# Whole normalized input and side-by-side in-projections in all later sub-layers of a two-layer decoder trunk

## The chip, the core and the metric

The kernel runs on one core of a Trainium2 chip. The metric is the device time of one execution in microseconds (us). The engines are named PE (TensorE, matmul; PEld is its weight load), DVE (VectorE), ACT (ScalarE), POOL (GpSimd) and SP (SyncE, which issues the loads).

## The reference

`x` is one sequence of 256 tokens with 1024 features, in float32. Two layers of three sub-layers each are applied, and a final RMSNorm. The sub-layers are numbered 0 to 5 in what follows.

```python
cond = silu(c)
for l in range(2):
    mod = cond @ ada_w[l] + ada_b[l]            # shift, scale, gate for each of 3 sub-layers
    h = rmsnorm(x, g) * (1 + scale) + shift     # modulate
    x = x + 0.5 * gate * swiglu(h)              # sub-layers 0 and 3: FFN, D_FF = 2816
    h = modulate(x)
    x = x + gate * (retention(h) if l == 0 else short_conv(h))   # sub-layers 1 and 4
    h = modulate(x)
    x = x + 0.5 * gate * swiglu(h)              # sub-layers 2 and 5: FFN
return rmsnorm(x, final_g)
```

`swiglu(h)` is `(silu(h @ w_gate) * (h @ w_up)) @ w_out`. `retention` projects to q, k, v and a gate, takes decayed scores of 4 heads against v, normalizes each head and multiplies by silu of the gate. `short_conv` multiplies two projections, filters the product with a causal 3-tap filter per feature, multiplies by a third projection and projects out.

## The kernel before

Features lie on the partitions: `x` is 8 blocks of 128 features x 256 tokens. Every float32 product is made exact enough by halves: `split_high` and `split_low` turn each load of weights (128 x 2048) into a high half (`hi`, an ACT cast, line 245) and a low half (`lo`, a subtraction on DVE or POOL, line 250), and the moving operand is split the same way. `product` then issues three half-products for each 128x128 weight block: hi x high, hi x low, lo x high. If the output is twice as wide as the operand (line 284), the first two are one matmul of 512 columns, whose two output halves are added later ("side by side", lines 285 and 289); otherwise they are two matmuls onto the same 256 columns (lines 287 to 289).

Every weight is used once, so the kernel is one stream of loads (SP queue), splits and matmuls. `weights()` keeps `AHEAD` = 4 loads in preparation; there are six `hi` and six `lo` tiles, two of each for a load. In between, 64 loads of `ada_w` are reduced on DVE (line 120) for the modulation of later sub-layers, paced so that they end in sub-layer 4. From the eleventh block of the first FFN on, the conditioning vector for these reductions lies in one of the four PSUM pairs (`kept`), which leaves three.

A later sub-layer does not wait for its own rms. `scaled` makes `h` = x * scale as soon as a residual is done, with the shift as two extra columns (so 258 columns, S1), and the first projection starts on `h`. `modulated` issues this first projection, then sums the squares over partitions with matmuls against ones (line 358), std on ACT (line 370) and r = 1/std on DVE (line 376). In the FFN and the short convolution all projections use `h`; `normalized` multiplies PSUM by r (line 325), and the shift enters behind it as a bias per feature. Only the retention makes the whole normalized input as well (`whole`: lines 437, 438, 331 and 332, x * r, scale and shift, split), into 8 tiles of the pool `slot`. Its first three projections (`BIASED`) use `h`, and all behind them use `whole`; its gates go side by side through `projected` (one half is copied by ACT, line 312, the other added by DVE, line 313).

The retention's `values` forms a head's four 128-feature blocks in two PSUM pairs, two blocks in each; `normalize` forms the rms of a head of one step earlier, and stands before `values` in the loop. For the first sub-layer `first_modulated` squares x in four pairs of blocks (line 476, three on DVE, one on POOL) and sums all eight blocks on PE. There the order on ACT, DVE and POOL is that of the program; elsewhere a scheduler orders each engine's instructions by program order and by the times at which it estimates that operands and buffers are ready.

## Time and profile before

| | us |
|---|---|
| median of 3 runs (lowest, highest) | 1095.13 (1094.88, 1095.41) |
| the profiled execution, its own time | 1094.71 |
| its span, first to last instruction | 1092.9 |
| PE busy in the span | 1067.8 |
| DVE busy | 830.8 |
| ACT busy | 578.0 |
| POOL busy | 391.0 |

The span is what the trace covers; the execution's own time has 1.8 us more around it. A PE that counts as busy may still be slower than it could be, since matmuls are pipelined and their bars overlap: its rate is read from the start times of matmuls that stand far apart.

### The profile page before, as it was taken

The page shows a single profiled execution, that of the slowest core. Times are in us where ns is not written, and L with a number is a line of the kernel's source. Part 1 is how long each engine was busy: PE and PEld are TensorE (multiplying, and loading weights), DVE is VectorE, ACT ScalarE, POOL GpSimd, SP SyncE. Part 2 cuts the span into 40 slices and gives each one's busy share as a digit, 9 for nine tenths or more (in the row PEclk, how much of TensorE's full clock was granted, in tenths as well). Part 3 has the DMA queues.
Part 4 walks back from the last instruction along what each step waited for, and adds up shares of the span by engine and source line. Part 5 has one row for each costly group of instructions (what it writes and reads, how often), then busy time and mean ns, then how long its engine had stood idle before and what let it go on. Part 6 is the DMA issues. An engine that isn't in the chain of part 4 may idle for free.

```text
span 1092.9 us, 19439 instructions
## 1 busy us (share of the span) xinstructions
PE 1067.8 (98%) x7706; PEld 1008.9 (92%) x7706; DVE 830.8 (76%) x1089; ACT 578.0 (53%) x923; POOL 391.0 (36%) x339
## 2 busy tenths in 40 slices
PE   8999999999998999999999999999999989999996
PEld 7999988999887889999988999998899989999985
DVE  6999776998558898887678878767798686666454
ACT  4364444663367655545555644545564484454442
POOL 0034355345354432332445133344411442323352
PEclk9999999999999999999999999999999999999998
DMA  9977779867555687777679767767885545553441
GB/s 344 364 275 275 295 280 314 314 239 296 208 221 198 227 308 274 268 277 261 219 267 324 300 249 297 266 223 264 305 317 210 190 156 191 173 188 123 156 133 39
DMA packets 44573, 268.51 MB, mean 246 GB/s; under 512 B 4801, under 2 KB 6977, under 8 KB 19906
## 3 DMA queue, kind: packets, MB, share of 16 engines
q1 hardware_dynamic: 43138, 266.56, 67.1%
q8 instruction: 60, 0.98, 0.4%
q10 hardware_dynamic: 1344, 0.71, 0.2%
q14 instruction: 31, 0.25, 0.1%
HBM read 266.20 MB, written 1.05 MB: 245 GB/s over the span
## 4 chain that ended last, share of the span: by engine, by line
PE 59%; DVE 2%; issue 0%; ACT 0%; DVEq 0%; ACTq 0%
PE ps L289 20%; PE ps L288 14%; PE ps L287 14%; PE ps L285 11%; DVE lo L250 1%; PE ps L358 0%; DVE rsum L511 0%; DVE h L412 0%; DVE raw L804 0%; DVE r L800 0%; DVE x L514 0%; ACT hi L245 0%; DVEq L877 0%; DVE x L516 0%; ACT std L370 0%
## 5 line engine op out<-in xcount | busy, mean ns | idle before, releaser
L250 DVE TENSOR_TENSOR lo<-raw,hi 128x1024 fp32r<-128x1024 f32 (+1 forms) x300 | 366.6, 1230 | 176.6 <-ACT hi L245 161.1
L245 ACT CAST hi<-raw 128x1024 fp32r<-128x1024 f32 (+2 forms) x408 | 377.7, 937 | 221.2 <-PE ps L288 123.3
L288 PE MATMUL ps<-h,hi 128*128 128x258 f32 (+1 forms) x1520 | 430.4, 283 | 1.7 <-DVE h L412 1.5
L287 PE MATMUL ps<-h,hi 128*128 128x258 f32 (+1 forms) x1520 | 430.5, 283 | 1.1 <-DVE sum L325 1.1
L289 PE MATMUL ps<-h,lo 128*128 128x258 f32 (+1 forms) x1520 | 430.5, 283 | 0.0
L250 POOL TENSOR_TENSOR lo<-raw,hi 128x384 fp32r<-128x384 f32 (+1 forms) x108 | 201.5, 1867 | 290.4 <-ACT hi L245 290.0
L288 PEld LDWEIGHTS ps<-h,hi 128*128 128x128 f32 x1520 | 288.7, 190 | 2.6 <-DVE h L412 1.3
L287 PEld LDWEIGHTS ps<-h,hi 128*128 128x128 f32 x1520 | 289.0, 190 | 1.8 <-ACT sg L586 0.7
L289 PEld LDWEIGHTS ps<-h,lo 128*128 128x128 f32 x1520 | 288.7, 190 | 0.0
L285 PE MATMUL ps<-act,hi 128*128 128x512 f32 x616 | 217.5, 398 | 0.6 <-DVE rsum L511 0.6
L289 PE MATMUL ps<-act,lo 128*128 128x256 f32 x704 | 197.8, 281 | 0.0
L332 POOL TENSOR_TENSOR act<-av,act 128x256 fp32r<-128x256 f32 x88 | 84.0, 957 | 251.2 <-ACT act L331 242.8
L120 DVE CUSTOM_DVE_ANT_0 raw<-raw,ps,misc 128x1024 f32<-128x1024 f32 x124 | 154.5, 1274 | 0.0
L285 PEld LDWEIGHTS ps<-act,hi 128*128 128x128 f32 x616 | 115.6, 188 | 29.4 <-DVE rsum L511 1.7
L289 PEld LDWEIGHTS ps<-act,lo 128*128 128x128 f32 x704 | 133.1, 189 | 0.3 <-DVE lo L250 0.3
L331 ACT CAST act<-av 128x256 fp32r<-128x256 f32 x88 | 35.5, 405 | 100.4 <-DVE av L590 78.3
L325 DVE TENSOR_TENSOR sum<-ps,r 128x516 f32<-128x516 f32 (+1 forms) x103 | 70.7, 690 | 16.1 <-PE ps L289 15.8
L590 DVE SCALAR_TENSOR_TENSOR av<-sum,sg 128x256 f32<-128x256 f32 x66 | 51.9, 786 | 17.8 <-ACT sg L589 17.8
L289 PE MATMUL ps<-whole,lo 128*128 128x256 f32 x208 | 58.5, 281 | 0.0
L589 ACT ACTIVATE sg<-sum 128x256 f32<-128x256 f32 x66 | 33.6, 509 | 26.3 <-DVE sum L325 25.9
L341 ACT ACTIVATE sq<-x 128x256 f32<-128x256 f32 x48 | 19.7, 416 | 51.6 <-DVE x L514 44.3
L348 POOL TENSOR_TENSOR acc<-acc,sq 128x256 f32<-128x256 f32 x32 | 28.0, 875 | 38.8 <-ACT sq L341 33.7
(132 smaller groups left out, 1296.2 us busy)
## 6 DMA issues: line engine op xcount, KB each, us to landing
raw<-in_ffn_in SPq DMA_DIRECT2D x80, 1024.0 KB, 4.9
raw<-in_ada_w SPq DMA_DIRECT2D x64, 1024.0 KB, 5.5
raw<-in_ffn_out SPq DMA_DIRECT2D x64, 704.0 KB, 4.2
raw<-in_ada_w SPq DMA_DIRECT2D x16, 512.0 KB, 6.8
raw<-in_ffn_in SPq DMA_DIRECT2D x16, 512.0 KB, 7.6
raw<-in_ret_g SPq DMA_DIRECT2D x8, 1024.0 KB, 5.1
raw<-in_ret_qk SPq DMA_DIRECT2D x8, 1024.0 KB, 5.1
raw<-in_ret_v SPq DMA_DIRECT2D x8, 1024.0 KB, 4.8
```

Source lines behind the costliest of these rows:

```text
L120: ins = nc.vector.tensor_tensor_reduce(out=w, in0=w, in1=state["cond"], scale=1.0, scalar=misc[:, C_ADAB + 72 * l + col:C_ADAB + 72 * l + ...
L245: nc.scalar.copy(out=hi, in_=raw[:, c:c + m])
L250: eng.tensor_tensor(out=lo, in0=raw, in1=hi, op=ALU.subtract)
L285: nc.tensor.matmul(out=ps, lhsT=hi, rhs=m.rearrange("p n s -> p (n s)"), start=start, stop=False)
L287: nc.tensor.matmul(out=ps, lhsT=hi, rhs=m[:, 0], start=start, stop=False)
L288: nc.tensor.matmul(out=ps, lhsT=hi, rhs=m[:, 1], start=False, stop=False)
L289: nc.tensor.matmul(out=ps[:, :n], lhsT=lo, rhs=m[:, 0], start=False, stop=stop)
L325: nc.vector.tensor_tensor(out=y[:, :, :n], in0=ps[:, :, :n], in1=r[:, :n].unsqueeze(1).to_broadcast([P, 2, n]), op=ALU.mult)
L331: hi = nc.scalar.copy(out=dst[:, 0], in_=src)
L332: lo = eng.tensor_tensor(out=dst[:, 1], in0=src, in1=dst[:, 0].bitcast(F32), op=ALU.subtract)
L589: nc.scalar.activation(out=sg, in_=y[:, 0, :S], func=AF.Silu, bias=y[:, 0, S:S + 1])
L590: nc.vector.scalar_tensor_tensor(out=av, in0=y[:, 1, :S], scalar=y[:, 1, S:S + 1], in1=sg, op0=ALU.add, op1=ALU.mult)
```

## The change

In all later sub-layers the whole normalized input is made, and every projection behind the third uses it side by side, without a bias. `ffn` and `short_conv` take the record `src` that the retention had, and go through `projected`. The pool `slot` grows from 22 to 30 tiles of 128 x 512; for that the scaled blocks of the first sub-layer (`xs`) come from it, and `cond` takes a tile of the pool of high halves. `values` puts a head's four blocks into one PSUM pair and is issued before the `normalize` of the head before. In the first sub-layer DVE and POOL each square two pairs, and pairs are added before PE sums them.

```diff
@@ -72,7 +72,7 @@
     wraw_p = ctx.enter_context(tc.tile_pool(name="wraw", bufs=5))
     whi_p = ctx.enter_context(tc.tile_pool(name="whi", bufs=6))
     wlo_p = ctx.enter_context(tc.tile_pool(name="wlo", bufs=6))
-    slot_p = ctx.enter_context(tc.tile_pool(name="slot", bufs=22))
+    slot_p = ctx.enter_context(tc.tile_pool(name="slot", bufs=30))
     xhl_p = ctx.enter_context(tc.tile_pool(name="xhl", bufs=1))
     tmp = ctx.enter_context(tc.tile_pool(name="tmp", bufs=2))
     psum = ctx.enter_context(tc.tile_pool(name="psum", bufs=4, space=bass.MemoryType.PSUM))
@@ -85,7 +85,7 @@
 
 
     misc = const.tile([P, C_END], F32, name="misc")
-    cond = const.tile([P, D], F32, name="cond")
+    cond = whi_p.tile([P, D], F32, name="cond", tag="hi")
     table = const.tile([P, T_END], F32, name="table")
     ones = const.tile([P, P], F32, name="ones")
     eps = const.tile([P, 1], F32, name="eps")
@@ -239,7 +239,7 @@
         c = w["done"]
         m = min(step, width - c)
         if c % SPLIT == 0:
-            hi, lo = whi_p.tile([P, SPLIT], F32R, name="hi"), wlo_p.tile([P, SPLIT], F32R, name="lo")
+            hi, lo = whi_p.tile([P, SPLIT], F32R, name="hi", tag="hi"), wlo_p.tile([P, SPLIT], F32R, name="lo")
             w["parts"].append((hi, lo))
         hi, lo = (part[:, c % SPLIT:c % SPLIT + m] for part in w["parts"][-1])
         nc.scalar.copy(out=hi, in_=raw[:, c:c + m])
@@ -471,17 +471,21 @@
             with tc.issue_after(conditioned.ins):
                 load_table(AF.Sqrt, ones)
             ps = banks()[:, 0, :S]
-            for i, pair in enumerate(x_pairs):
-                sq = tmp.tile([P, 2, S], F32, name="sq2", tag="rot" if i % 2 else "sum")
-                (nc.gpsimd if i == 1 else nc.vector).tensor_tensor(out=sq, in0=pair, in1=pair, op=ALU.mult)
-                total([sq[:, 0, :], sq[:, 1, :]], ps, i == 0, i == KB // 2 - 1)
+            for i in range(2):
+                sqs = []
+                for j, eng in ((2 * i, nc.vector), (2 * i + 1, nc.gpsimd)):
+                    sq = tmp.tile([P, 2, S], F32, name=f"sq{j}", tag="rot" if i else "sum")
+                    eng.tensor_tensor(out=sq, in0=x_pairs[j], in1=x_pairs[j], op=ALU.mult)
+                    sqs.append(sq)
+                (nc.gpsimd if i else nc.vector).tensor_tensor(out=sqs[0], in0=sqs[0], in1=sqs[1], op=ALU.add)
+                total([sqs[0][:, 0, :], sqs[0][:, 1, :]], ps, i == 0, i == 1)
             std = tmp.tile([P, S], F32, name="std")
             nc.scalar.activation(out=std, in_=ps, func=AF.Sqrt, bias=eps, scale=1.0 / D)
             fill(FILL)
             for k in range(KB):
                 ada_reduce(l, s, k, ada.pop(), True)
                 if k % 2 == 0:
-                    pair = tmp.tile([P, 2, S], F32, name=f"xs{k}", bufs=1)
+                    pair = in_halves(slot(F32, "xs"))
                 xs = pair[:, k % 2, :]
                 nc.scalar.activation(out=xs, in_=x[k], func=AF.Copy, scale=scale_t[l][s][:, k:k + 1])
                 raw, width, w = load(2)
@@ -574,30 +578,33 @@
                     nc.tensor.matmul(out=out, lhsT=lo, rhs=h[k][:, 0], start=False, stop=stop)
         return [ps.rearrange("p (n s) -> p n s", s=S) for ps in pss]
 
-    def ffn(n, h, r, begun=None):
+    def ffn(n, src=None, h=None, r=None):
         act = []
 
-        def activate(ps):
-            n = h[0].shape[-1]
-            y = normalized(ps, r, n)
+        def activate(y, bias):
             sg = tmp.tile([P, S], F32, name="sg")
             av = tmp.tile([P, S], F32, name="av", bufs=3)
-            if n == S:
-                nc.scalar.activation(out=sg, in_=y[:, 0, :S], func=AF.Silu)
+            silu(y, 0, bias, sg)
+            if bias is None:
                 nc.vector.tensor_tensor(out=av, in0=sg, in1=y[:, 1, :S], op=ALU.mult)
             else:
-                nc.scalar.activation(out=sg, in_=y[:, 0, :S], func=AF.Silu, bias=y[:, 0, S:S + 1])
                 nc.vector.scalar_tensor_tensor(
-                    out=av, in0=y[:, 1, :S], scalar=y[:, 1, S:S + 1], in1=sg, op0=ALU.add, op1=ALU.mult
+                    out=av, in0=y[:, 1, :S], scalar=bias[1][:, :1], in1=sg, op0=ALU.add, op1=ALU.mult
                 )
             t = in_halves(slot(F32R, "act"))
             split(t, av, nc.gpsimd)
             act.append(t)
 
-        for ps in first_projections(h) if n == 0 else [begun]:
-            activate(ps)
+        if n == 0:
+            for ps in first_projections(h):
+                activate(normalized(ps, r, S), None)
+        else:
+            src["whole"] = whole(n, src["r"])
         while len(act) < FB:
-            activate(projections(h))
+            if n:
+                activate(*projected(src))
+            else:
+                activate(normalized(projections(h), r, S), None)
             if n == 0 and len(act) == KEEP:
                 kept = banks().rearrange("p n c -> p (n c)")
                 nc.scalar.copy(out=kept, in_=cond)
@@ -684,16 +691,15 @@
         def values(hd, sc):
 
             blocks = []
+            ps = banks()
+            for b in range(4):
+                c = slice(b * P, (b + 1) * P)
+                o = ps[:, b // 2, b % 2 * S:(b % 2 + 1) * S]
+                nc.tensor.matmul(out=o, lhsT=v[hd][0][:, c], rhs=sc[:, :S], start=True, stop=False)
+                nc.tensor.matmul(out=o[:, P:], lhsT=v[hd][1][:, c], rhs=sc[:, S:S + P], start=False, stop=True)
             for half in range(2):
-                ps = banks()
-                for i in range(2):
-                    c = slice((2 * half + i) * P, (2 * half + i + 1) * P)
-                    nc.tensor.matmul(out=ps[:, i, :S], lhsT=v[hd][0][:, c], rhs=sc[:, :S], start=True, stop=False)
-                    nc.tensor.matmul(
-                        out=ps[:, i, P:S], lhsT=v[hd][1][:, c], rhs=sc[:, S:S + P], start=False, stop=True
-                    )
                 t = slot(F32, "o")
-                nc.scalar.copy(out=t.rearrange("p (n s) -> p n s", s=S), in_=ps[:, :, :S])
+                nc.scalar.copy(out=t, in_=ps[:, half, :])
                 blocks += [t[:, :S], t[:, S:]]
             sq = [square(blocks[0]), square(blocks[1])]
             acc = added(sq[0], sq[1])
@@ -728,10 +734,10 @@
             run()
             if step == 0:
                 sc = {hd: scores(hd) for hd in range(HEADS)}
+            if 0 <= step - 1 < HEADS:
+                raw_o[step - 1] = values(step - 1, sc[step - 1])
             if 0 <= step - 2 < HEADS:
                 o[step - 2] = normalize(step - 2, *raw_o[step - 2])
-            if 0 <= step - 1 < HEADS:
-                raw_o[step - 1] = values(step - 1, sc[step - 1])
             while len(gated) // 4 in o and len(gated) // 2 < len(gates):
                 apply()
         before_residuals(n)
@@ -739,16 +745,20 @@
         for d in range(2, KB):
             output(n, d, [(weights(), 0, gated)])
 
-    def short_conv(n, h, r, begun):
+    def short_conv(n, src):
         gated = []
-
-        def taps(d, y, cv):
-            u = tmp.tile([P, S], F32, name="u", tag="sg")
+        src["whole"] = whole(n, src["r"])
+
+        def taps(y, bias, cv):
             z = tmp.tile([P, S], F32, name="z", tag="av", bufs=3)
-            nc.scalar.activation(out=u, in_=y[:, 1, :S], func=AF.Identity, bias=y[:, 1, S:S + 1])
-            nc.vector.scalar_tensor_tensor(
-                out=z, in0=y[:, 0, :S], scalar=y[:, 0, S:S + 1], in1=u, op0=ALU.add, op1=ALU.mult
-            )
+            if bias is None:
+                nc.vector.tensor_tensor(out=z, in0=y[:, 0, :S], in1=y[:, 1, :S], op=ALU.mult)
+            else:
+                u = tmp.tile([P, S], F32, name="u", tag="sg")
+                nc.scalar.activation(out=u, in_=y[:, 1, :S], func=AF.Identity, bias=bias[1][:, :1])
+                nc.vector.scalar_tensor_tensor(
+                    out=z, in0=y[:, 0, :S], scalar=bias[0][:, :1], in1=u, op0=ALU.add, op1=ALU.mult
+                )
             tap = [misc[:, C_CONV + i * KB + d:C_CONV + i * KB + d + 1] for i in range(3)]
             nc.scalar.activation(out=cv, in_=z, func=AF.Copy, scale=tap[2])
             for i, sh in ((1, 1), (0, 2)):
@@ -761,14 +771,12 @@
             if d % 2 == 0:
                 pair = slot(F32, "conv")
             convs.append(pair[:, d % 2 * S:(d % 2 + 1) * S])
-            taps(d, normalized(projections(h) if d else begun, r), convs[d])
+            taps(*projected(src), convs[d])
         for d2 in range(KB // 2):
-            y = normalized(projections(h), r)
+            y, _ = projected(src)
             for i in range(2):
                 yc = y[:, i, :S]
-                nc.vector.scalar_tensor_tensor(
-                    out=yc, in0=yc, scalar=y[:, i, S:S + 1], in1=convs[2 * d2 + i], op0=ALU.add, op1=ALU.mult
-                )
+                nc.vector.tensor_tensor(out=yc, in0=yc, in1=convs[2 * d2 + i], op=ALU.mult)
                 t = in_halves(slot(F32R, "yg"))
                 split(t, yc, nc.gpsimd if d2 < KB // 2 - 1 else nc.vector)
                 gated.append(t)
@@ -783,15 +791,16 @@
 
     for n, (l, s) in enumerate(sublayers):
         if n == 0:
-            ffn(n, *first_modulated())
+            ffn(n, None, *first_modulated())
             continue
         h, r, std, begun = modulated()
+        src = {"h": h, "r": r, "begun": begun, "used": 0}
         if s != 1:
-            ffn(n, h, r, begun)
+            ffn(n, src)
         elif l % 2 == 0:
-            retention(n, {"h": h, "r": r, "begun": begun, "used": 0})
+            retention(n, src)
         else:
-            short_conv(n, h, r, begun)
+            short_conv(n, src)
     std = rms([norm.pop("last")], D, norm.pop("bank")[:, 0, :S])
     r = tmp.tile([P, S], F32, name="r")
     with tc.manual_schedule(engines={mybir.EngineType.DVE, mybir.EngineType.Pool}):
```

## Rows read from the trace of the kernel before

**Rows 1.** The page, part 1: engine, busy us (share of the span), instructions.

```profile
PE 1067.8 (98%) x7706; PEld 1008.9 (92%) x7706; DVE 830.8 (76%) x1089; ACT 578.0 (53%) x923; POOL 391.0 (36%) x339
```

**Rows 2.** Timeline of PE: start us, duration us, line, output and operands, form.

```profile
351.01 0.58 PE L285 MATMUL ps<-whole,hi 128*128 128x512 f32 x1
...
367.85 0.39 PE L285 MATMUL ps<-og,hi 128*128 128x512 f32 x1
...
419.32 0.47 PE L287 MATMUL ps<-h,hi 128*128 128x258 f32 x1
...
541.58 0.40 PE L285 MATMUL ps<-act,hi 128*128 128x512 f32 x1
...
609.89 0.47 PE L287 MATMUL ps<-h,hi 128*128 128x258 f32 x1
...
732.71 0.40 PE L285 MATMUL ps<-act,hi 128*128 128x512 f32 x1
...
800.99 0.47 PE L287 MATMUL ps<-h,hi 128*128 128x258 f32 x1
...
897.50 0.47 PE L287 MATMUL ps<-h,hi 128*128 128x258 f32 x1
...
1019.21 0.39 PE L285 MATMUL ps<-act,hi 128*128 128x512 f32 x1
```

**Rows 3.** PE's waits: line <- what ended it: us, times, longest.

```profile
PE ps L691 <- ACT std L370: 2.2, 2, 1.2
...
PE ps L285 <- DVE sum L313: 1.9, 1, 1.9
...
PE ps L287 <- ACT whole L331: 1.1, 1, 1.1
...
PE ps L288 <- DVE whole L332: 0.9, 1, 0.9
```

**Rows 4.** Timeline of DVE: the reciprocals of sub-layers 1 to 4, the last whole blocks.

```profile
215.19 1.74 DVE L376 RECIPROCAL r<-std 128x256 f32<-128x256 f32 x1
...
230.63 0.76 DVE L332 TENSOR_TENSOR whole<-xr,whole 128x256 fp32r<-128x256 f32 x2
...
421.02 1.75 DVE L376 RECIPROCAL r<-std 128x256 f32<-128x256 f32 x1
...
613.99 1.75 DVE L376 RECIPROCAL r<-std 128x256 f32<-128x256 f32 x1
...
803.37 1.75 DVE L376 RECIPROCAL r<-std 128x256 f32<-128x256 f32 x1
```

**Rows 5.** Windows: us, PE, PEld, DVE, ACT, POOL busy; PE clock, DMA share, GB/s.

```profile
429.00:435.00 6.00, 6.00 (x52) 6.00 (x51) 6.00 (x7) 3.10 (x5) 3.14 (x2) 1.00 0.94 377
...
905.00:911.00 6.00, 6.00 (x52) 6.00 (x51) 3.92 (x5) 2.98 (x5) 0.73 (x1) 1.00 0.49 175
```

**Rows 6.** Groups by form: count | busy us, mean ns | idle before.

```profile
L120 DVE CUSTOM_DVE_ANT_0 raw<-raw,ps,misc 128x1024 f32<-128x1024 f32 x124 | 154.5, 1274 | 0.0
...
L332 DVE TENSOR_TENSOR whole<-xr,whole 128x256 fp32r<-128x256 f32 x8 | 4.6, 615 | 0.0
...
L438 ACT ACTIVATE xr<-xr,mod,sc 128x256 f32<-128x256 f32 x8 | 4.5, 597 | 3.7 <-POOL xr L437 3.6
...
L313 DVE TENSOR_TENSOR sum<-ps,sum 128x512 f32<-128x512 f32 x5 | 3.3, 669 | 0.0
...
L312 ACT COPY sum<-ps 128x512 f32<-128x512 f32 x5 | 2.9, 579 | 0.0
...
L331 ACT CAST whole<-xr 128x256 fp32r<-128x256 f32 x8 | 2.8, 399 | 0.0
...
L437 DVE TENSOR_TENSOR xr<-x,r 128x256 f32<-128x256 f32 x4 | 2.1, 550 | 0.0
```

**Rows 7.** Timeline of PE and POOL at the start.

```profile
6.36 1.04 POOL L476 TENSOR_TENSOR sq<-x 128x512 f32<-128x512 f32 x1 [5.39 <-DMA x<-in_x]
...
8.23 4.23 PE L358 MATMUL ps<-sq,ones 128*128 128x256 f32 x12
```

## The prediction

> **What bounds the kernel now.** I read the page's busy shares first, then the order of TensorE's (PE's) matmuls in time, then what PE waited for, then VectorE (DVE) around the places where a sub-layer begins. The reader is to see in [rows 1] that PE is busy 98% of the span, while DVE has 76% and ScalarE (ACT) 53%. So time comes off only where PE needs less time for the same product, or where one of its few idle gaps closes.
>
> The second view gives PE's rate, stage by stage. After the rms matmuls, a later FFN runs 21 in-projections of 16 steps each, 336 steps; a step is one 128x128 weight block against all 256 tokens in three half-products. Its duration is the time between the first of these matmuls and the first of the out-projection, over 336 [rows 2]: in sub-layer 2, (541.58 - 419.32) / 336 = 0.3639 us; in 3, (732.71 - 609.89) / 336 = 0.3655; in 5, (1019.21 - 897.50) / 336 = 0.3622. The retention's last three gate projections use the other form, one 512-column matmul and one of 256, on the whole normalized input: (367.85 - 351.01) / 48 = 0.3508 us a step. Both forms stream nearly the same columns (774 against 768); the second has two matmuls and two weight loads where the first has three.
>
> The third view, PE's waits, is to show how few gaps there are: the retention's value products wait 2.2 us for ACT's std, the projection behind them 1.9 us for DVE's sum, and the first product on the whole input 1.1 and 0.9 us [rows 3].
>
> **The change, part by part.** *In-projections.* In sub-layers 2, 3 and 5, 19 of 22 projections (304 steps) take the side-by-side form, in the short convolution 9 of 12 (144 steps): 66 projections, 1056 steps. From the rates above: 304 x (0.3639 - 0.3508) = 4.0 us, 304 x 0.0147 = 4.5, 304 x 0.0114 = 3.5, and for the convolution at sub-layer 2's rate 144 x 0.0131 = 1.9. Sum **-13.8 us**. The bounds are all 1056 steps at the least and at the greatest difference: 12.0 and 15.5.
>
> The Trainium skill (TensorE: Matmul & The Clock Gate, Back-to-back issue gap) gives an isolated matmul N/2.4 + 2.5 ns, so three of 258 columns would take 330 ns and the pair of 512 and 256 columns 325; by it the saving is 5 ns a step, 5.3 us in all. The trace has 362 to 366 and 351 ns; the rows decide, but the rule is a rival.
>
> Their evacuation changes too. DVE multiplied by r; now ACT copies one half out of PSUM (0.579 us) and DVE adds the other (0.669 us, [rows 6]). DVE's work stays about the same, ACT gets 66 x 0.579 = 38 us, less what the dropped biases save. I cost this at nothing: ACT is idle 47% of the span [rows 1], and PE goes on into another PSUM pair meanwhile. Were that cover gone, each of the 66 projections could lose up to one copy, 38 us. Behind such a copy, which waits for PE, stand on ACT the casts of the next weights, and DVE's low halves wait for those.
>
> *The whole input, four times more.* For each of the 8 blocks of x: a product with r (DVE and POOL in turn), scale and shift on ACT, a cast on ACT, a subtraction on DVE. By [rows 6] that is 4 x 0.550 + 8 x 0.615 = 7.1 us of DVE and 8 x (0.597 + 0.399) = 8.0 us of ACT for a sub-layer. It must be done between r (the reciprocal) and the fourth projection, the first that reads it. The first three still use the old h and cover it. The retention shows how long this takes amid the other work: r was ready at 215.19 + 1.74 = 216.93 us and the last block at 230.63 + 0.76 = 231.39, 14.5 us later [rows 4], and PE waited 2.0 us [rows 3].
>
> The same 14.5 us, set at each new place: the fourth projection starts 32 steps after the first matmul behind the rms [rows 2], 11.6 to 11.7 us, and needs its eighth block 7/8 x 16 x 0.3508 = 4.9 us later. Sub-layer 2: r at 421.02 + 1.75 = 422.77, blocks done at 437.3, needed at 419.32 + 11.64 + 4.9 = 435.9: 1.4 us late. Sub-layer 3: r at 615.74, done 630.2, needed 609.89 + 11.70 + 4.9 = 626.5: 3.7 late. Convolution: r at 805.12, done 819.6, needed 800.99 + 11.64 + 4.9 = 817.5: 2.1 late [rows 2, 4]. Sub-layer 5 starts this at about 897.5; no adaLN reductions are left, and DVE is busy 3.92 of 6 us soon after (against 6.00 of 6 in sub-layer 2) [rows 5]: I take 0. Sum **+7.2 us**. What is late behind it: DVE's 7.1 us push back the low halves of weights and the SwiGLU products. About two loads of weights stand ready ahead of PE (six tiles, two a load), so some 11 us, and I charge nothing for that.
>
> Bounds: one adaLN job is two DVE reductions of 1.274 us [rows 6]. If one of them less falls into the stretch, the chain is 2.5 us shorter, and only sub-layer 3 is late, by 1.2. In sub-layer 2 DVE has no idle time in this stretch [rows 5], and the SwiGLU products and a second job stand in it. With 4 us more each, the lateness is 5.4 + 7.7 + 6.1 and, in sub-layer 5, some 4, together 23 us.
>
> *The retention's values.* A head's four blocks now share one PSUM pair instead of two, and they come ahead of the previous head's rms. Both waits of [rows 3] are for a free pair: the second half of the values waited until std had read the pair of the rms, and the next projection until the sum had been evacuated. With one pair less in use I take both as gone: **-4.1 us**. Bounds: nothing (the wait moves to the rms's own pair) and 4.1 with up to another microsecond behind it. The later normalization of a head lies under the next projections; were it late, the gated blocks of the last head would hold up the out-projection.
>
> *Squares of x.* PE's rms for the first sub-layer was 16 passes; the last 12 ran from 8.23 to 12.46 us, 0.353 each [rows 7], and the start waited for them. Now they are 8, and 4 are left behind the last addition. That addition is on POOL, behind a second square of 1.04 us [rows 7]: squares until about 8.5 to 9.2, the addition of two tiles at 1.04 to twice that, 9.5 to 11.3, then 4 x 0.353 = 1.4: 10.9 to 12.7 against 12.46. I take **-0.4 us**, bounds -1.5 and +0.3. DVE's first addition waits for POOL's square, and its next square is queued behind it.
>
> *The rest.* Slots go from 22 to 30, which is just 22 activations plus 8 whole blocks, so the whole input needs no freed activation. The conditioning vector now sits in one of the six high-half tiles until the eleventh block of the first FFN, which shortens the lead of the weights there by half a load, 8 steps or 2.9 us of some 14. I cost it at nothing; if it shows, it is at most that 2.9 us once. No transfer is added, enlarged or moved to another queue; SP's loads only follow buffers that DVE frees.
>
> **Sum:** -13.8 + 7.2 - 4.1 - 0.4 = -11.1 us. The profiled execution took 1094.71 us, of which 1092.9 is the span; the median shown is 1095.13, 0.42 more. So 1084.0 us.
>
> **The rivals.** *The whole input is ready in time.* If the blocks come 2.5 us sooner, 1.2 us of lateness remains: -17.1, 1078.0. For it speaks that PE's own waiting gives DVE time; against it that the retention, with the same work, did stall.
>
> *The whole input arrives far too late: slower.* One mechanism: DVE in the stretch behind r, full in sub-layers 2 and 4. The gains are 18.3 us. Against 7.2 us of lateness at 14.5, each microsecond more of this chain costs 3 to 4 us, so from about 3 us more the change loses. At 4 us more, 23 - 18.3 = +4.7, 1099.8. For it speaks the 6.00 of 6 us; against it, that whole blocks are issued ahead of the activations, and so pass them.
>
> *The step saves only what fewer columns give.* 774 to 768 columns is 0.8%: 1056 x 0.3639 x 0.008 = 3.0 us instead of 13.8, so -0.3 in all, 1094.8. (The Trainium skill's issue gap, as above, makes it 5.3 us and the sum -2.6, 1092.5.) Against it stand 48 steps at 0.3508.
>
> *The PSUM wait only moves.* The rms of the values needs a pair just as before: -7.0, 1088.1.
>
> **How the numbers follow.** The forecast (lateness of 3 to 12 us, the rest as summed) gets 0.59, ready in time 0.14, too late 0.13, the small step 0.06, the moved wait 0.08. The predicted time is 1084.0. The range reaches from the first rival, 1077.5, to 1094.5, which leaves out most of the slow case and little else. A difference under 0.2% (2.2 us) can hardly be told from none; faster is below 1092.9. Faster: 0.59 + 0.14 + 0.08 less a little of the forecast's upper tail, 0.80; same: the small step and that tail, 0.08; slower: 0.12.
>
> **What the profile after would show.** Right: in sub-layers 2, 3 and 5 a step near 0.351 us; PE waiting 0 to 4 us for whole blocks (DVE or ACT) at the fourth projection of four sub-layers, most in sub-layer 3; the two retention waits gone; std of the first sub-layer at about 12 us or before. Wrong: PE waiting for low halves of weights some 15 us behind each r; a step at 0.36 or above; a wait for std or a sum still in front of the value products or the gates; PE idle within an FFN because ACT's copies stand behind casts that wait for PE.

## The result, and the profile after

The changed kernel takes 1088.74 us (median of five runs, 1085.63 to 1091.05) against 1095.13 (five runs, 1094.74 to 1095.81) beside it: a ratio of 0.9942, 95% interval 0.9922 to 0.9963. That is 6.4 us faster. The forecast was 1084.0 in a range from 1077.5 to 1094.5. The profiled execution, 1085.63 us with a span of 1083.8, was the quickest of the five; its trace gives 9.1 us against the 1094.71 of before, where the sum of the prediction gave 11.1.

The page's first part, of the kernel after, to be held against [rows 1]:

```profile
PE 1052.3 (97%) x6642; PEld 947.2 (87%) x6642; DVE 841.7 (78%) x1137; ACT 623.7 (58%) x1048; POOL 411.2 (38%) x357
```

PE is still the bound. It has 1064 matmuls fewer, about one for each of the 1056 steps, and 15.5 us less busy time, but the span is only 9.1 shorter: PE's idle time grew by the other 6.4. ACT has 46 us more (38 of copies and 4 x 8.0 of whole blocks were costed, less what dropped biases save), and DVE 11 more.

The timeline of PE after (start us, us, line, operands, form, and in brackets the idle time before it and who ended it) answers to [rows 2]:

```profile
338.30 0.60 PE L358 MATMUL ps<-acc,ones 128*128 128x256 f32 x2
...
340.50 0.50 PE L285 MATMUL ps<-whole,hi 128*128 128x512 f32 x1 [1.60 <-ACT std L370]
...
349.78 1.22 PE L358 MATMUL ps<-acc,ones 128*128 128x256 f32 x2 [3.36 <-POOL acc L348]
...
420.44 0.47 PE L287 MATMUL ps<-h,hi 128*128 128x258 f32 x1
...
432.20 0.39 PE L285 MATMUL ps<-whole,hi 128*128 128x512 f32 x1
...
435.28 0.50 PE L285 MATMUL ps<-whole,hi 128*128 128x512 f32 x1 [0.84 <-DVE whole L332]
...
437.49 0.50 PE L285 MATMUL ps<-whole,hi 128*128 128x512 f32 x1 [0.54 <-DVE whole L332]
...
539.56 0.39 PE L285 MATMUL ps<-act,hi 128*128 128x512 f32 x1
...
607.87 0.47 PE L287 MATMUL ps<-h,hi 128*128 128x258 f32 x1
...
619.72 0.40 PE L285 MATMUL ps<-whole,hi 128*128 128x512 f32 x1
...
622.67 0.50 PE L285 MATMUL ps<-whole,hi 128*128 128x512 f32 x1 [0.70 <-DVE whole L332]
...
624.56 0.50 PE L285 MATMUL ps<-whole,hi 128*128 128x512 f32 x1 [0.21 <-DVE whole L332]
...
627.17 0.50 PE L285 MATMUL ps<-whole,hi 128*128 128x512 f32 x1 [0.72 <-DVE whole L332]
...
727.76 0.39 PE L285 MATMUL ps<-act,hi 128*128 128x512 f32 x1
...
814.53 0.50 PE L285 MATMUL ps<-whole,hi 128*128 128x512 f32 x1 [2.23 <-DVE whole L332]
...
892.97 0.47 PE L287 MATMUL ps<-h,hi 128*128 128x258 f32 x1
...
904.83 0.40 PE L285 MATMUL ps<-whole,hi 128*128 128x512 f32 x1
...
1010.22 0.39 PE L285 MATMUL ps<-act,hi 128*128 128x512 f32 x1
```

Read as before, from the first step behind the rms to the first out-projection step, the FFNs take 119.12, 119.89 and 117.25 us, where [rows 2] give 122.26, 122.82 and 121.71. In sub-layer 5, where nothing is late, a side-by-side step takes (1010.22 - 904.83) / 304 = 0.3467 us.

PE's waits after, to be held against [rows 3] (us in all, times, longest):

```profile
PE ps L285 <- DVE whole L332: 5.2, 6, 2.2
PE ps L358 <- POOL acc L348: 3.4, 1, 3.4
...
PE ps L285 <- ACT std L370: 1.6, 1, 1.6
...
PE ps L287 <- ACT whole L331: 1.0, 1, 1.0
...
PE ps L288 <- DVE whole L332: 0.9, 1, 0.9
```

The first row is the lateness that was forecast. The last two are the retention's own whole input, unchanged. The second and third are new and stand in the retention, where two waits should have gone.

Between these places the two traces can be laid over each other. What each stretch gained or lost, against the term of the sum for it:

| stretch | forecast, us | measured, us |
|---|---|---|
| start to the first product of sub-layer 1 (206.43 before, 206.12 after) | -0.4 | -0.3 |
| from there to 419.32 / 420.44: retention and its rms | -4.1 | +1.4 |
| FFN of sub-layer 2, in-projections | -4.0 + 1.4 | -3.1 |
| FFN of sub-layer 3, in-projections | -4.5 + 3.7 | -2.9 |
| convolution, in-projections | -1.9 + 2.1 | +0.2 |
| FFN of sub-layer 5, in-projections | -3.5 | -4.5 |
| out-projections, final norm | 0 | +0.1 |
| sum | -11.1 | -9.1 |

One row has the wrong sign: the retention. The -0.3 of the first row isn't that of the squares: the first product of weights starts at 14.44 us before and at 14.40 after, and the other 0.25 us come within the first FFN (experiment 6).

### The profile page after: what moved, and what is told of

Same layout as the page of the kernel before. It is cut to its first block, busy times and chain, and to the rows that moved or that the text cites. A ratio compares the mean times of both kernels' runs of the same rounds, so it can differ in the third digit from the quotient of the medians.

```text
span 1083.8 us, 17516 instructions
## 1 busy us (share of the span) xinstructions
PE 1052.3 (97%) x6642; PEld 947.2 (87%) x6642; DVE 841.7 (78%) x1137; ACT 623.7 (58%) x1048; POOL 411.2 (38%) x357
## 4 chain that ended last, share of the span: by engine, by line
PE 54%; DVE 7%; issue 1%; ACT 0%; DVEq 0%; ACTq 0%
PE ps L285 32%; PE ps L289 18%; DVE lo L250 2%; PE ps L288 2%; PE ps L287 2%; DVE raw L120 1%; DVE whole L332 1%; DVE xr L437 1%; DVE r L376 0%; DVE h L412 0%; DVE sum L325 0%; DVE av L591 0%; DVE rsum L515 0%; DVE raw L813 0%; PE ps L358 0%
## 5 line engine op out<-in xcount | busy, mean ns | idle before, releaser
L285 PE MATMUL ps<-whole,hi 128*128 128x512 f32 x1136 | 397.5, 394 | 6.8 <-DVE whole L332 5.2
L289 PE MATMUL ps<-whole,lo 128*128 128x256 f32 x1264 | 353.7, 280 | 0.0
L285 PEld LDWEIGHTS ps<-whole,hi 128*128 128x128 f32 x1136 | 213.2, 188 | 56.8 <-DVE whole L332 7.4
L289 PEld LDWEIGHTS ps<-whole,lo 128*128 128x128 f32 x1264 | 239.5, 189 | 0.2
L287 PE MATMUL ps<-h,hi 128*128 128x258 f32 (+1 forms) x464 | 131.9, 284 | 1.0 <-DVE sum L325 1.0
L288 PE MATMUL ps<-h,hi 128*128 128x258 f32 (+1 forms) x464 | 131.4, 283 | 1.4 <-DVE h L412 1.2
L289 PE MATMUL ps<-h,lo 128*128 128x258 f32 (+1 forms) x464 | 130.2, 281 | 0.0
L288 PEld LDWEIGHTS ps<-h,hi 128*128 128x128 f32 x464 | 87.9, 190 | 2.6 <-DVE h L412 2.2
L287 PEld LDWEIGHTS ps<-h,hi 128*128 128x128 f32 x464 | 87.6, 189 | 1.5 <-ACT sg L318 1.1
L289 PEld LDWEIGHTS ps<-h,lo 128*128 128x128 f32 x464 | 87.6, 189 | 0.0
L313 DVE TENSOR_TENSOR sum<-ps,sum 128x512 f32<-128x512 f32 x71 | 48.6, 685 | 22.7 <-ACT sum L312 22.7
L589 DVE TENSOR_TENSOR av<-sg,sum 128x256 f32<-128x256 f32 x79 | 51.2, 651 | 13.0 <-ACT sg L318 13.0
```

What stands on the lines that cost most here:

```text
L285: nc.tensor.matmul(out=ps, lhsT=hi, rhs=m.rearrange("p n s -> p (n s)"), start=start, stop=False)
L287: nc.tensor.matmul(out=ps, lhsT=hi, rhs=m[:, 0], start=start, stop=False)
L288: nc.tensor.matmul(out=ps, lhsT=hi, rhs=m[:, 1], start=False, stop=False)
L289: nc.tensor.matmul(out=ps[:, :n], lhsT=lo, rhs=m[:, 0], start=False, stop=stop)
L313: nc.vector.tensor_tensor(out=y[:, :, :S], in0=ps[:, :, :S], in1=y[:, :, :S], op=ALU.add)
L589: nc.vector.tensor_tensor(out=av, in0=sg, in1=y[:, 1, :S], op=ALU.mult)
```

## The experiments

Each kernel was timed beside the kernel before on the same chip, which took 1095.12, 1095.36 and 1094.9 us there. The ratios are to those runs.

**1. The retention alone, undone and done.** The theory: its two waits for a PSUM pair did not go but moved, and the clock fell behind the longer of them; that costs what the steps gain too little. The rival: the steps are at fault.

The first kernel is the changed one with the retention as before:

```diff
-            ps = banks()
-            for b in range(4):
-                ...
             for half in range(2):
+                ps = banks()
+                for i in range(2):
+                    ...
@@
-            if 0 <= step - 1 < HEADS:
-                raw_o[step - 1] = values(step - 1, sc[step - 1])
             if 0 <= step - 2 < HEADS:
                 o[step - 2] = normalize(step - 2, *raw_o[step - 2])
+            if 0 <= step - 1 < HEADS:
+                raw_o[step - 1] = values(step - 1, sc[step - 1])
```

> The changed kernel with the retention's values and its loop order as before; the whole input and the side-by-side projections stay. Theory A (the retention's part of the change costs time: PE waits 1.6 us for std and 3.4 us for the last head's squares, and the granted clock halves behind the second wait, for longer in the slower runs): retention back to about 206 us, clock 0.997 again, runs within 1 us of each other, about 1083.5 us. Theory B (the spread and the lower clock come from the denser in-projections, and the retention is innocent): 1086 to 1091 us as the changed kernel, clock 0.992 to 0.995.

Measured: 1087.88 us (1087.16 to 1089.41), ratio 0.9938 (0.9924 to 0.9953). The waits came back as they were, and no stretch of the trace ahead of the final norm has the lower clock, as theory A said:

```profile
PE ps L698 <- ACT std L370: 2.2, 2, 1.2
...
PE ps L285 <- DVE sum L313: 1.9, 1, 1.9
```

The time did not fall to theory A's figure; it lies in theory B's range, and by the medians it can't be told from the changed kernel's. In this trace the steps of sub-layers 2, 3 and the convolution were slower (experiment 3).

The second is the reverse: the lines that this diff removes, put into the kernel before in place of those that it adds, and nothing else of the change.

> The kernel before with the retention's part of the change alone (values in one pair, ahead of the rms). Theory A: the same two waits and the fall of the clock, so 1097 to 1100 us with a spread of some us, clock below 0.997. Theory B: the waits of 2.2 and 1.9 us go and nothing takes their place, 1091 to 1093 us, clock 0.997.

Measured: 1098.24 us (1097.14 to 1098.73), ratio 1.0032 (1.0019 to 1.0044), as theory A expected: the part costs 3.1 us by itself. The same two waits stand in its PE's waits:

```profile
PE ps L358 <- POOL acc L348: 3.4, 1, 3.4
...
PE ps L285 <- ACT std L370: 1.6, 1, 1.6
```

Not all of the 3.1 us is explained by them. In this trace the clock is also low from 231.1 to 234.6 us, ahead of all values, which costs about 1.5 us and which the trace of the kernel before doesn't have; whether the part brings that about is not shown (experiment 3).

**2. The wait of the last head.** The 3.4 us are PE standing at the rms of the last head's values, whose squares are late. The timeline of ACT in the changed kernel shows why:

```profile
339.97 0.48 ACT L370 ACTIVATE std<-ps,eps 128x256 f32<-128x256 f32 x1
342.37 0.19 ACT L331 CAST h<-mod 128x2 fp32r<-128x2 f32 x1 [1.92 <-DVE mod L120]
342.58 1.28 ACT L318 ACT_TABLE_LOAD   x1
343.87 0.72 ACT L318 ACTIVATE gate<-sum 128x256 f32<-128x256 f32 x2
344.50 1.06 ACT L702 COPY o<-ps 128x512 f32<-128x512 f32 x2
```

PE had ended these values where the rms of 338.30 begins. Their copy out of PSUM is at 344.50, six us later, behind other work in ACT's queue: in front of it stand a cast ahead of which ACT is idle for 1.92 us, until an adaLN reduction of DVE has ended, a table load of 1.28 us and a SiLU. The squares and their sums follow the copy, and PE's rms follows them. So the rms of the last head was put one step later:

```diff
+            hd = HEADS - 1 if step == HEADS + 2 else step - 2
-            if 0 <= step - 2 < HEADS:
-                o[step - 2] = normalize(step - 2, *raw_o[step - 2])
+            if 0 <= hd < HEADS and step != HEADS + 1:
+                o[hd] = normalize(hd, *raw_o[hd])
```

> The changed kernel with the last head's rms and normalization one projection later. Theory A, with the wait put down to the rms standing too soon behind its values: the 3.4 us wait goes, the clock does not halve, about 1082 to 1083 us with a small spread. Rival: ACT's copies of the values are late because they stand behind instructions that wait for DVE's adaLN reductions, so that PE waits elsewhere (for a free PSUM pair) and the time stays within 2 us of the changed kernel.

Measured: 1084.59 us (1082.92 to 1089.38), ratio 0.9914 (0.9888 to 0.9939). The 3.4 us wait is gone from its waits, the mean clock of the trace is 0.998, and no stretch ahead of the final norm has the lower level; the wait for std (1.6 us) stays, and one of 0.7 us for a sum is new. The median is above the 1082 to 1083 expected and the four times spread over 6.5 us, so the trace has to decide. The stretch of the table in which the retention lies, from the first product of sub-layer 1 to the first step behind the next rms, can be read from the starts of these two in each trace (us, computed from the records):

```
before                            212.89
changed, first and second trace   214.32  216.75
undone, first and second trace    213.45  213.47
alone, in the kernel before       215.36
last rms later                    210.27
```

With the last rms later it is 4.0 us shorter than in the quicker trace of the changed kernel, and 2.6 shorter than before. That bears the theory out: 3.4 us of wait and 1.6 us of half clock went, and 0.7 us of wait came. The second trace of the changed kernel and that of the part alone hold, besides, the low clock at 230 us.

**3. The same program again.** The five times of the changed kernel spread over 5.4 us, those of the kernel before beside them over 1.1. So the changed kernel and the one with the retention undone were run again, on another chip. (There the sixteen times of the kernel before spread over 6.4 us, so the spread is not the change's alone.)

> The changed kernel once more, for a second trace and more times. In its first trace a side-by-side step took 0.347 us nearly everywhere in sub-layers 2 to 5, in the kernel with the retention undone 0.3535 in 2, 3 and 4. Theory D (two paces of the same step, which an execution falls into by chance at the start of a stage): this trace shows another mix of 0.347 and 0.3535 than the first, and the times spread over 1085 to 1091 us again. Theory E (the pace belongs to the program, by where its tiles lie): the same paces stage by stage as in the first trace.

> The kernel with the retention undone once more. Theory D: another mix of paces than 0.3535 in sub-layers 2, 3 and 4, and an execution at 0.347 throughout near 1083 us. Theory E: 0.3535 there again, and 1087 to 1089 us.

Measured: 1091.01 us for the changed kernel (ten runs, 1088.94 to 1093.65; ratio 0.9964, 0.9948 to 0.9981) and 1088.46 with the retention undone (seven runs, 1087.23 to 1091.62; 0.9944, 0.9926 to 0.9962). Side by side, undoing the retention gives 2.5 us, beside the 3.1 that doing it alone cost in experiment 1.

Two things differ between the two traces of the changed kernel. (The two with the retention undone differ in a third, the start: experiment 6.) The first is the clock. Windows of the changed kernel's first trace (us, then busy time of PE, PEld, DVE, ACT, POOL; granted clock, DMA share, GB/s):

```profile
349.60:353.00 3.40, 3.22 (x9) 2.75 (x10) 2.67 (x2) 2.85 (x4) 1.80 (x2) 0.50 0.01 2
351.00:353.00 2.00, 2.00 (x8) 1.71 (x7) 1.46 (x1) 1.90 (x3) 0.40 (x1) 0.50 0.02 4
353.00:355.00 2.00, 2.00 (x13) 1.72 (x13) 2.00 (x4) 0.29 (x1) 0.00 (x0) 0.99 0.00 0
700.00:720.00 20.00, 20.00 (x117) 17.50 (x116) 15.04 (x21) 11.35 (x19) 6.32 (x6) 1.00 0.79 296
```

and of its second:

```profile
230.40:233.80 3.40, 3.07 (x14) 3.08 (x15) 1.53 (x4) 2.98 (x7) 0.10 (x1) 0.50 0.99 376
349.90:356.70 6.80, 5.64 (x17) 4.79 (x18) 5.40 (x6) 3.81 (x5) 2.77 (x3) 0.50 0.05 13
700.00:720.00 20.00, 20.00 (x116) 17.32 (x115) 15.60 (x23) 10.97 (x17) 6.45 (x5) 1.00 0.66 234
```

Around the end of the 3.4 us wait the granted clock falls to 0.50, 1.2 GHz: PE is busy in every moment from 351 to 355 us, and issues 8 matmuls in the first half of it and 13 in the second, at full clock. In the first trace that lasts 3.4 us (349.6 to 353.0). In the second it lasts 6.8 (349.9 to 356.7), and another 3.4 us stand at 230.4 to 233.8, at the retention's waits for its own whole input, which are the same in both. Each us in which PE works at this level loses about half a us, so the second execution loses about (3.07 + 5.64 - 3.22) / 2 = 2.7 us more. By the starts of sub-layer 2's fourth projection (432.20 and 434.59) it is 2.4.

The second is the pace of the step, in the last window of each at full clock. From the timeline of PE in the second trace, sub-layer 3's first and last side-by-side steps:

```profile
622.06 0.40 PE L285 MATMUL ps<-whole,hi 128*128 128x512 f32 x1
...
732.00 0.40 PE L285 MATMUL ps<-act,hi 128*128 128x512 f32 x1
```

That is 109.94 us, where the first trace has 727.76 - 619.72 = 108.04: the same instructions, 1.9 us more. Mean distance of two steps in the traces, ns (computed from the records, not a view):

```
                 sub-layer 2   3    conv    5
changed, first       347      347   347    347
changed, second      347      353   353    347
undone, first        353      353   353    347
undone, second       353      353   353    347
rms later (exp. 2)   353      347   353    347
four on h (exp. 4)   347      347   347    347
```

There are only these two paces, 346.7 and 353.3 ns. At the first each step's matmuls start about 232 and 115 ns apart; at the second the distances rotate through 232, 235 and 241 and 114 to 120. Most in-projections keep the pace that they begin with; out-projections, and the convolution in three of the traces with the cover of experiment 4, change it on the way. The kernel before has both too: its out-projections of sub-layers 2, 3 and 5, in the same form, run at 347 in about their first quarter and at 353 in the rest. What chooses the pace is open: both executions with the retention undone took the same pace at the same stages on two chips, which speaks for the order of instructions or the moment of the start; the changed kernel did not, which speaks against the program alone. The faster window even moves more over DMA (0.79 against 0.66). If all 1056 steps changed pace, it would be some 7 us.

Together these two account for the second trace: behind the first trace by 2.4 us at the fourth projection of sub-layer 2, by 4.2 at the end of sub-layer 3's projections (1.9 of them there), by 5.3 in sub-layer 5, where both have 347 ns.

**4. Cover for the whole input.** Is the 5.2 us wait the chain from r to the last block? Then one more projection on the old h covers it. The constant also holds for the retention.

```diff
-BIASED = 3
+BIASED = 4
```

> The changed kernel with four projections on the old h instead of three, so that the whole blocks have 5.8 us more. Theory C (the blocks are late by a fixed 2 to 4 us behind r): the waits for whole blocks, 1.7, 2.1 and 2.4 us in sub-layers 2 to 4 and 2.4 us in the retention, all go, at a price of 5 x 16 steps x 0.0165 us = 1.3 us, so about 7 us faster than the changed kernel. Rival (DVE has no time to spare there, and whatever it does first makes something else late): PE waits for low halves or for PSUM instead, no change or 1 us slower.

Measured: 1080.22 us (1079.76 to 1081.89), ratio 0.9869 (0.9855 to 0.9884), 8.5 below the changed kernel. PE's waits have no row for a whole block any more, the retention's own included. The largest that are left behind the start:

```profile
PE ps L358 <- POOL acc L348: 2.3, 1, 2.3
PE ps L288 <- DVE h L412: 1.8, 3, 1.0
PE ps L285 <- DVE sum L325: 1.7, 1, 1.7
PE ps L285 <- ACT std L370: 1.6, 1, 1.6
```

Waits of 5.2 + 1.0 + 0.9 us went and one of 1.7 came (a pair of PSUM in sub-layer 2 not yet evacuated). This execution also had the quicker pace in all four stages, so not all of the 8.5 us is due to the waits. Beside the changed kernel's first trace, at the same pace, the profiled execution is 5.9 us shorter: 2.4 us came off sub-layer 3's projections and 1.5 off the convolution's, nothing off those of sub-layer 2, where the new wait stands, and 2.3 off the stretch with the retention.

Both cures together, this diff and that of experiment 2:

> Both mendings together: four projections on the old h, and the last head's rms one projection later. If their gains are independent: the 2.5 us wait for the last head's squares and the 1.7 us that half the clock costs behind it go from the four-biased kernel's 1080.2, about 1076 us. Rival: the wait moves to another place of the retention, 1079 to 1081.

Measured: 1079.65 us (1077.37 to 1080.06), ratio 0.9853 (0.9829 to 0.9878), no better than the cover alone by more than its spread, as the rival said. The 2.3 us wait for the squares has become one of 2.3 us for DVE's sum, again for a PSUM pair.

**5. What the retention's waits hang on.** To see whether the adaLN reductions in DVE's queue hold up std and sum, they were kept out of the six loads ahead of the retention's out-projection, on top of both cures.

```diff
-        if any(o - BEFORE <= n < o + BEHIND for o in outputs):
+        if any(o - BEFORE <= n < o + BEHIND for o in outputs) or outputs[1] - 6 <= n < outputs[1]:
```

> The same with no adaLN load begun in the retention's last six projections before its output. Theory F (ACT's copies of the values and the sums are late because DVE reduces adaLN weights ahead of them, so that PE lacks a PSUM pair): the waits for std (1.6 us) and for the sum (0.9 to 1.7 us) go, 2 to 3 us less than the kernel before it. Rival: the reductions are caught up in the out-projection and make the next sub-layer late, no gain or a loss.

Measured: 1079.93 us (1078.21 to 1081.74), ratio 0.986 (0.9835 to 0.9886). Its PE's waits:

```profile
PE ps L288 <- DVE h L412: 2.8, 3, 1.9
...
PE ps L285 <- ACT std L370: 1.0, 1, 1.0
PE ps L285 <- DVE sum L313: 0.9, 1, 0.9
```

The cause was right: std fell from 1.6 to 1.0 and sum from 2.3 to 0.9. Nothing was gained, as the rival said: the reductions now stand behind the out-projection, the next sub-layer's h is late (2.8 us), and the clock was at 0.50 for 3.4 us behind it. This trace also started its first product of weights 2.1 us later than that of both cures (experiment 6).

With the cover of experiment 4, the retention was once undone, by the diff of experiment 1, and once changed by half: one pair, but with the previous head's rms ahead of the values as before, and the last head's one step later.

```diff
+            hd = HEADS - 1 if step == HEADS + 2 else step - 2
+            if 0 <= hd < HEADS and step != HEADS + 1:
+                o[hd] = normalize(hd, *raw_o[hd])
             if 0 <= step - 1 < HEADS:
                 raw_o[step - 1] = values(step - 1, sc[step - 1])
-            if 0 <= step - 2 < HEADS:
-                o[step - 2] = normalize(step - 2, *raw_o[step - 2])
```

> Four projections on the old h, and the retention's values and order as before. If the retention's part of the change costs some 3 us wherever it stands (as it did alone), this is 2 to 3 us below the four-biased kernel's 1080.2, about 1077.5, with the clock never halved. Rival (what it costs is set by what stands around it, and the four-biased kernel has hidden it): 1080.

> Four projections on the old h; a head's values in one PSUM pair, but the rms of the head before stands first again, and the last head's rms comes one projection later. Theory (the one pair is right, and the new order is what lost the gain, since std then begins only behind the values and holds the pair that the next gate projection needs): the waits for std of 1.6 us and of 2.2 us are both gone, and 2 us below the kernel with both mendings (1079.65), about 1077 to 1078. Rival (the sum's evacuation behind DVE's reductions is what PE waits for in either order): another wait for DVE's sum of 1 to 2 us, 1079 to 1080.

Measured: 1082.14 us (1081.33 to 1083.07, ratio 0.9885, 0.987 to 0.99) for the first. The expectation was wrong: with the cover, the old form waits 3.1 us for DVE's sum, not 1.9, and 6.8 us at the lower clock (347.6 to 354.4) go with it. So what the retention's part is worth depends on what stands around it: by the medians, undoing it gains 2.5 us in the changed kernel and loses 1.9 with the cover, there between two chips and with intervals that touch. The second took 1078.21 us (1077.48 to 1080.08, ratio 0.9854, 0.9836 to 0.9872), the lowest median of all and close to what was expected, but not in the way that was expected: a wait for std is left in the retention, and 3.4 us at 0.50 of the clock go with it.

```profile
PE ps L285 <- ACT std L370: 2.7, 1, 2.7
```

**6. Squares of x undone**, with the four squares and sixteen passes of before.

```diff
-            for i in range(2):
-                ...
-                (nc.gpsimd if i else nc.vector).tensor_tensor(out=sqs[0], in0=sqs[0], in1=sqs[1], op=ALU.add)
-                total([sqs[0][:, 0, :], sqs[0][:, 1, :]], ps, i == 0, i == 1)
+            for i, pair in enumerate(x_pairs):
+                ...
+                total([sq[:, 0, :], sq[:, 1, :]], ps, i == 0, i == KB // 2 - 1)
```

> The changed kernel with the squares of x as before. If the squares in pairs save what was forecast, PE's first weight product starts 0.4 us later here than in the changed kernel's traces (14.40 us, counted from the span's start); if POOL's square and addition use up what PE saves, within 0.1 us of it, apart from when x lands.

Measured: 1090.34 us in one run, which says nothing of tenths. The start of its trace has std at 12.83 us and the first product of weights at 14.71, where the changed kernel's first trace has 12.49 and 14.40. That looks like the 0.3 us of the expectation. But the other traces have the same two forms of the squares too (us, computed from the records):

```
                               std     first product of weights
squares as before
  before                       12.56   14.44
  retention alone              11.66   13.53
  squares undone               12.83   14.71
squares in pairs
  changed, both traces         12.49   14.40    12.45   14.33
  undone, both traces          12.56   14.78    14.92   16.80
  the six of experiments 2, 4 and 5   std 12.03 to 14.33, first product 14.30 to 16.44
```

The traces of one form differ by more than 0.3 us, and the earliest start of all is one with the squares as before. They differ first in when x lands: the second square starts between 5.39 and 7.17 us. And in the two latest starts POOL's addition, on which std now waits, took 2.17 us instead of the 1.26 or 1.27 of the other eight. So a gain from the squares isn't shown.

## Why the prediction was right, and which step failed

**The bound** was right: time came off PE's own work, and every loss found is a gap, a slow clock or a slower pace on PE.

**The step of the in-projections** was the right mechanism and sized too small. The four stages gained 10.3 us with 7.0 us of lateness among them, so 17.3 us for 1056 steps, 16.4 ns each, where the term had 13.8 us. The reason is the 0.3508 us taken from the retention's gates in [rows 2]. The first of those 48 steps stands behind a wait and an rms, and took 0.54 us; the next row of that timeline, in the trace of the kernel before, is

```profile
351.55 0.40 PE L285 MATMUL ps<-whole,hi 128*128 128x512 f32 x1
```

From there the other 47 take (367.85 - 351.55) / 47 = 0.3468 us: the quicker pace, which the changed kernel's first execution had too. With it, and with 0.3633, 0.3650 and 0.3617 for the old steps of sub-layers 2, 3 and 5 (computed from the records, their first step left out as well), the term would be 304 x (0.0165 + 0.0182 + 0.0149) + 144 x 0.0165 = 17.5 us. At 353.3 ns it would be 304 x (0.0100 + 0.0117 + 0.0084) + 144 x 0.0100 = 10.6 us. Both lie outside its bounds of 12.0 and 15.5, so these were too narrow on both sides: one slow step was spread over 48, and one stage couldn't show that a step has two paces. The rival of the small step is refuted, and so is the rule of the Trainium skill (TensorE: Matmul & The Clock Gate, Back-to-back issue gap) as it was weighed: its gap of an isolated matmul, taken for this stream, gave an estimate of 325 ns a step and 5 ns saved, against 347 or 353 measured and 8 to 18 saved.

**The lateness** was right, within 0.2 us in sum, though by stage it was off by up to 1.1. The timeline of DVE after, to be held against [rows 4]:

```profile
422.13 1.75 DVE L376 RECIPROCAL r<-std 128x256 f32<-128x256 f32 x1
...
438.09 0.76 DVE L332 TENSOR_TENSOR whole<-xr,whole 128x256 fp32r<-128x256 f32 x2
...
611.97 1.75 DVE L376 RECIPROCAL r<-std 128x256 f32<-128x256 f32 x1
...
626.16 1.81 DVE L332 TENSOR_TENSOR whole<-xr,whole 128x256 fp32r<-128x256 f32 x2
...
798.42 1.74 DVE L376 RECIPROCAL r<-std 128x256 f32<-128x256 f32 x1
...
814.07 0.75 DVE L332 TENSOR_TENSOR whole<-xr,whole 128x256 fp32r<-128x256 f32 x2
```

From the end of each reciprocal to the end of the last block it is 15.0, 14.3 and 14.7 us, for 14.5 assumed. What PE lost, counted from start to start of the steps around the waits above (each less 0.35), is 1.9, 2.6, 2.5 and 0 us: 7.0, for 1.4, 3.7, 2.1 and 0, 7.2. In sub-layer 3 it is less than forecast, and PE there has three steps of the next projection ahead of the seventh block: five steps lie between the waits that end at 624.56 and 627.17, where a block has two. The slower rival, a chain 3 us longer, did not come, and the one of a whole input in time did not either; experiment 4 is what it would look like.

**The retention's values: this step failed.** The prediction said "With one pair less in use I take both as gone: -4.1 us". The trace shows +1.4, experiment 1 +3.1 by itself. Three things were missed. The pairs freed were not enough: the wait for std is still there with 1.6 us, now in front of the next gate, which needs a pair as well; the prediction had named that as a sign of being wrong. The new order puts the rms behind the values, and the last head's squares wait for a copy that stands six us behind others on ACT (mended in experiment 2, the stretch came out 2.6 us shorter than before); the prediction looked at what the later normalization would hold up (the gated blocks), not at PE waiting at the rms itself. And with the wait of 3.4 us came the half clock, which no gap ahead of the final norm brought in the trace of before. The rival "the PSUM wait only moves" was right in kind and, at 0 us, still too kind; that the median lies near its 1088.1 us is chance, since other terms make up the sum.

**The squares** (-0.4) are not shown. Std starts at 12.49 us, where the prediction wanted about 12 or before and the kernel before has 12.56; between traces of one form this start moves by more than the term, and in the two traces with the slow addition, where x landed late as well, it is some 2 us later (experiment 6).

**The parts costed at nothing** cost nothing. ACT's copies took 577 ns and DVE's additions 685, by the groups of the kernel after (count | busy us, mean ns | idle before):

```profile
L313 DVE TENSOR_TENSOR sum<-ps,sum 128x512 f32<-128x512 f32 x71 | 48.6, 685 | 22.7 <-ACT sum L312 22.7
...
L312 ACT COPY sum<-ps 128x512 f32<-128x512 f32 x71 | 41.0, 577 | 0.0
```

DVE idles 22.7 us for these copies, and PE waits for none of it: no wait for the low half of a weight has grown, and among the in-projections behind the third PE waits for whole blocks alone.

**From the profiled execution to the median** the prediction added 0.4 us, the difference of before. After, it is 3.1: the profiled execution was the quickest, and executions differ in clock and pace. The miss of 4.7 us in the median is made of the retention (+5.5), the steps of the quick execution (-3.5), 0.0 in the small terms, and 2.7 of this. That the profiled execution came within 2 us of the sum (-9.1 for -11.1) is partly luck, since the first two errors have opposite signs. The last part isn't settled: experiment 3 shows by windows what clock and pace did between two traces, but not what chooses the pace, and the run at the median has no trace.

## What to carry to other kernels

When a buffer's holders become fewer, follow the next thing that needs one, and follow the chain of the moved work through each engine's queue to the point where the busiest engine stands at it. An operand that arrives late can be covered: one more projection on the old one removed all of its waits for 16 slower steps a sub-layer, though a wait for PSUM took its place in one of them. Before the difference of two steps is multiplied by a thousand, leave the first step behind a wait out of its rate, and take the rate from several stages and executions.

## What the runs showed of the hardware

The same stream of a 512-column and a 256-column matmul, at a granted clock of 1.00, runs at 347 or at 353 ns a step and can keep its pace for a hundred us and more; one program took either in different executions. What selects it was not found.

In the retention a single PE wait of 3.4 us came with 3.4 us at 1.2 GHz in one execution and with 6.8 in another, the first 0.2 or 1.2 us of them still within the wait. Waits of 2.3 us (experiment 4) and 2.7 (experiment 5, the last kernel) came with 3.4 us of it, another of 2.3 us (both cures) with none. Two waits of 1.0 or 1.1 and 0.9 us near 230 us came with 3.4 us of it in some executions (three of the traces) and with none in others, the kernel before among them. So a gap's price isn't its length: with half of PE's time at the low level added, the 3.4 us wait cost about 5.0 or 6.2.
